# A decoder layer on one Trainium2 core: gather and scatter of the experts' tokens as two-part float32r products, four experts at a time

## The chip, the core and the metric

The kernel runs on one core of a Trainium2 chip. The core has a matrix engine (TensorE, in the profile PE, with PEld for the loading of its weights), VectorE (DVE), ScalarE (ACT), GpSimd (POOL), SyncE (SP) and 16 DMA engines that bring data from the chip's memory (HBM). Each engine runs its own queue of instructions in order and waits for the others by semaphores. The metric is the device time of one execution, in microseconds, and smaller is better. Three runs of the kernel before took 1217.1, 1217.46 and 1218.18 us, with a median of 1217.46.

## The reference

The layer works on 256 tokens of 2048 features, all in float32. It runs three mixers (pooling, sparse attention, cross attention), gates them, adds the projected sum to x, and then adds a mixture of 16 experts. The change touches the last part alone, which is:

```python
x = x + hierarchical_moe(rms_norm(x, g_ffn), ...)

# in hierarchical_moe, h: [1, 256, 2048]
w = pg_top * pe_top / jnp.sum(pe_top, axis=-1, keepdims=True)
e_id = g_top[..., None] * EXPERTS_PER_GROUP + e_local
combine = jnp.einsum('bsk,bske->bse', w, jax.nn.one_hot(e_id, N_EXPERTS))
a = jnp.einsum('bsd,edf->bsef', h, w_e_gate)
b = jnp.einsum('bsd,edf->bsef', h, w_e_up)
act = jax.nn.silu(a) * b * combine[..., None]
return jnp.einsum('bsef,efd->bsd', act, w_e_down)
```

Each token has two experts, both out of one group of four. `combine` is zero for the others, so the kernel computes each expert for its own tokens only. The weights of each expert are three float32 matrices of 2048 x 512 or 512 x 2048, 4 MiB each, and 192 MiB for all sixteen.

## The kernel before

**The stages.** Until about 725 us the kernel computes the mixers and the output projection. Their products take activations and weights as two float32r parts, high and low (lines 268 to 270: high times high, high times low, low times high; `split_evac`, lines 113 to 115, makes the parts with a copy on ACT and a subtraction on DVE). Then comes a short router, which ranks the logits and gives each token a place in the lists of its two experts (`slot`, counted from 1, 0 where an expert is not chosen), and after it the expert stage: eight pairs of experts, one after the other (`pair`, line 953). A pair has 128 slots, 64 for each of its two experts. An expert with more tokens than 64 would need further rounds (line 1073).

**A pair.** `pick` (line 894) compares `slot` with 1 to 64 and so makes a selection matrix [token, slot], multiplied by a factor of the token. `Gather` (line 927) multiplies x with the selection that carries the factor `r2` (1 / rms), in plain float32, and so gets the pair's tokens transposed, two of the 16 k-tiles of 128 features at a step (line 946, called line 951 where the program order is kept); DVE multiplies by the gain (line 947). `gemm` (line 963) runs gate and up, 8 weight tiles each, with the gathered tokens as the stationary operand. Sigmoid and two products make `sg`, which is transposed (line 998) into `aT`. The down product (line 1037) takes 8 more weight tiles in four column parts. `scatter` (line 1007) copies each part out (`ob`, line 1009) and multiplies it with the transposed selection `pwT` that carries the combine weights, also in plain float32 (line 1013); DVE adds the result to `y` (line 1015). The first pair gathers while it uses its gate weights, because all tokens must be there first. Of each later pair, four of eight gather steps come before and behind the transposes of `sg` in the pair ahead of it, and the rest beside its own gate product.

**The weights.** SP loads them in the order of use, one tile of 1 MiB per DMA (`prefetch`, line 731, and `load`, line 189). A load waits until the last product that read the same buffer is done. The buffers form a ring: four that held hT (`wh`), `NEX` of a pool of their own (`we`), four of the raw weights (`wr`) and two that held merged activations (`wm`). With NEX = 8 the ring has 18 buffers. For the first pass two more are there, `mx1`, which later hold `y`. Two tiles of the first pair (`late`, line 727) have buffers of their own. So 22 tiles are loaded before the first one is used up, and 170 follow as buffers come free.

**The order.** The program is written in the order above, and a scheduler with a model of the engines' times sets the order of each engine's queue from it. Only instructions that are pinned with `keep_in_program_order` stay as written: the loads, and the gather and gate products of the first pair.

Of the kernel before, what the change touches and what calls it, by code (L numbers as in the profile page):

```python
# [11 lines left out]
F32 = mybir.dt.float32  # L12
# [8 lines left out]
P = 128  # L21
# [10 lines left out]
NEX = 8  # L32
# [21 lines left out]
def layer_kernel(tc, x, xT, memT, pos, cst, band, gains, bgate, wmem, wxq, widx, wkqvp, wpg, wgb, wo, wr, we, out):  # L54
# [26 lines left out]
    class Quads:  # L81
        """High and low parts of a [K, tokens] operand, four k-tiles to a tile."""
# [67 lines left out]
    class RowRstd:  # L150
        """1 / rms of the tokens, from the transposed activations: squares summed over the k-tiles,
        then over the partitions by a product with ones."""
# [28 lines left out]
    def gain_split(src, gc, dst, q, ks=slice(0, 4)):  # L181
        """src: [P, 4, S], rows [512 q, 512 q + 512) of the transposed activations."""
        for k in range(ks.start, ks.stop):
            g = cs[:, gc + 4 * q + k : gc + 4 * q + k + 1]
            hi, lo = dst.q[q][:, 0, k], dst.q[q][:, 1, k]
            pin(A.activation(hi, src[:, k], AF.Copy, scale=g))
            pin(V.scalar_tensor_tensor(lo, src[:, k], g, hi, op0=ALU.mult, op1=ALU.subtract))
# [25 lines left out]
    # the weights in the order of their use: [P, k-tiles, n] in DRAM  # L213
# [6 lines left out]
    def feeder():  # L220
        """Loads the weights and splits them into two float32r parts, two k-tiles at a time."""
# [28 lines left out]
    def chunk(n, groups, rate=1, name=None, step=None):  # L250
        """groups: list of (k-tiles, operand, done); n output columns."""
# [27 lines left out]
    def warm(n, z, cols, ps):  # L279
        """Products of zeros that nobody reads: the array's clock is up when the next ones come."""  # L280
# [142 lines left out]
    def head_rstd(srcs, H, name):  # L423
        """srcs[t]: [P, H*HD] -> [P, NT, H] of 1/rms."""
# [12 lines left out]
    def transposes(srcs, dst, engine=None):  # L437
        """srcs: list of [P, 128] blocks; dst [P, n, 128] written through one bank (n <= 4)."""
# [6 lines left out]
    def softmax(ps, nk, bias, out):  # L445
        """ps: [P, 2, nk] logits of two heads; out gets the normalised probabilities in SBUF."""
# [74 lines left out]
    def rotary(dst, src, H, half, tl, t, sub=None):  # L521
        """dst, src: [P, H, 2*half]; tl: four [P, half] tables (cos g1, sin g2, cos g2, sin g1)."""
# [262 lines left out]
    def route_in(n, t, ac):  # L785
# [9 lines left out]
        if n < 3:  # L795
            # four k-tiles side by side in column groups of the array
# [42 lines left out]
    c_w, wk = pool("work", side="right")  # L839
    # two tiles of the first weights stay where later the results of their products go  # L840
# [22 lines left out]
    # rank of a logit in its group of four, equal ones in the order of their places; the logits are  # L863
    # those up to the token's positive factor r2; group 0 holds the group logits
# [18 lines left out]
    # place of a token in its expert's list, counted from 1; 0 where the expert is not chosen  # L883
# [10 lines left out]
    def pick(wp, pr, slot_, name, f, bufs=1):  # L894
        """[token, slot] selection of the pair's tokens, times the token's factor f(t, expert)."""
        v = wp.tile([P, NT, P], F32, tag=name, name=name, bufs=bufs)
        for t in range(NT):
            for e in range(2):
                k = 2 * pr + e
# [267 lines left out]
```

## Time and profile before

| | |
|---|---|
| median of three runs | 1217.46 us |
| span of the profiled execution, first to last instruction | 1215.5 us |
| what lies around the span, as the difference of these two | 1.96 us |
| TensorE busy | 1193.3 us, 98% of the span |
| VectorE, ScalarE, GpSimd busy | 546.6, 400.4 and 30.2 us |
| moved by DMA | 340.35 MB, 280 GB/s in the mean |
| expert stage | about 725 to 1207 us |

The profile holds one execution, and it gives a span and no other time of that execution. A busy share of TensorE counts the time in which at least one product is under way, and products overlap in its pipeline: the length of one instruction is not what it costs in a row of many. What it costs there is the distance from one start to the next, which the timeline shows where it merges a run of like instructions and gives their count. A float32 product stands in the trace as two instructions, and a float32r product as one.

### The profile page before, as it was taken

The numbers are of one execution on the slowest core, as the hardware profiler recorded it, in microseconds if no ns is written. First come the engines' busy times: TensorE is split into PE (matmuls) and PEld (weight loads), VectorE is DVE, ScalarE is ACT, GpSimd is POOL, SyncE is SP. The second block draws the span as 40 slices with busy tenths as digits, with TensorE's granted clock in tenths as the row PEclk, the third lists the DMA queues.
The fourth block names the chain that finished last, engine by engine and source line by source line (L and its number), as shares of the span: only waits on it lengthen the run. The fifth ranks groups of instructions, "written<-read, shape, count | busy, mean of one in ns | idle before, by whom it ended". The sixth has DMA issues, their size and how long they took to land. (4 is left out here: it accounts for less than half of the span.)

```text
span 1215.5 us, 15075 instructions
## 1 busy us (share of the span) xinstructions
PE 1193.3 (98%) x6079; PEld 814.7 (67%) x6079; DVE 546.6 (45%) x905; ACT 400.4 (33%) x604; POOL 30.2 (2%) x33
## 2 busy tenths in 40 slices
PE   8999999999999999999999999999999999999996
PEld 5788887888788888888887774545454545453533
DVE  7877469856465565565563541222121212121201
ACT  7765664456544444444444430100000000000000
POOL 4200000000000000000000000000000000000000
PEclk9999999999999999999999999999999999999998
DMA  9646454544745565555797488899999999999951
GB/s 379 208 149 216 173 181 145 201 165 158 256 161 207 183 215 192 206 193 206 300 360 308 173 311 324 338 379 426 405 425 380 426 427 425 422 425 425 427 225 72
DMA packets 49901, 340.35 MB, mean 280 GB/s; under 512 B 5665, under 2 KB 6305, under 8 KB 10401
## 3 DMA queue, kind: packets, MB, share of 16 engines
q1 hardware_dynamic: 46512, 329.83, 70.0%
q0 software_dynamic: 1728, 7.15, 1.7%
q10 hardware_dynamic: 1584, 2.34, 0.5%
q8 instruction: 50, 0.82, 0.3%
q14 instruction: 27, 0.21, 0.0%
HBM read 337.20 MB, written 2.10 MB: 279 GB/s over the span
## 5 line engine op out<-in xcount | busy, mean ns | idle before, releaser
L115 DVE TENSOR_TENSOR wl<-rawt,wh 128x1024 fp32r<-128x1024 f32 (+1 forms) x240 | 292.3, 1220 | 211.5 <-ACT wh L114 210.7
L114 ACT ACTIVATE wh<-rawt 128x1024 fp32r<-128x1024 f32 (+1 forms) x240 | 251.0, 1048 | 296.9 <-PE acc L270 291.4
L269 PE MATMUL acc<-wl,hT 128*128 128x512 f32 (+1 forms) x640 | 249.7, 390 | 0.7 <-DVE wl L115 0.7
L270 PE MATMUL acc<-wh,hT 128*128 128x512 f32 (+1 forms) x640 | 247.3, 387 | 0.0
L268 PE MATMUL acc<-wh,hT 128*128 128x512 f32 (+1 forms) x640 | 228.5, 390 | 0.0
L269 PEld LDWEIGHTS acc<-wl,hT 128*128 128x128 f32 x640 | 120.2, 188 | 25.1 <-DVE wl L115 1.1
L270 PEld LDWEIGHTS acc<-wh,hT 128*128 128x128 f32 x640 | 120.2, 188 | 23.1
L268 PEld LDWEIGHTS acc<-wh,hT 128*128 128x128 f32 x640 | 119.2, 188 | 23.5 <-issue 0.3
L972 PE MATMUL gu<-we,xg 128*64 128x512 f32 x464 | 108.1, 596 | 0.0
L1015 DVE TENSOR_TENSOR y<-y,sm 128x512 f32<-128x512 f32 (+1 forms) x58 | 38.9, 670 | 134.7 <-PE sm L1013 134.7
L972 PEld LDWEIGHTS gu<-we,xg 128*64 128x64 f32 x464 | 33.1, 137 | 58.7 <-issue 56.9
L1009 ACT ACTIVATE ob<-dn 128x512 f32<-128x512 f32 (+1 forms) x33 | 19.3, 585 | 157.6 <-PE dn L1037 153.0
L946 PEld LDWEIGHTS sm<-pg,x 128*128 128x128 f32 x448 | 53.5, 192 | 21.5 <-issue 21.5
L1013 PE MATMUL sm<-ob,pwT 128*128 128x512 f32 (+1 forms) x132 | 63.8, 605 | 0.5 <-ACT ob L1009 0.5
L947 DVE TENSOR_TENSOR xg<-sm,cs 128x256 f32<-128x256 f32 x64 | 26.6, 423 | 72.5 <-PE sm L946 51.9
L946 PE MATMUL sm<-pg,x 128*128 128x128 f32 x448 | 58.7, 280 | 0.0
L972 PE MATMUL gu<-wr,xg 128*64 128x512 f32 x216 | 51.5, 595 | 0.0
L269 PE MATMUL acc<-wl,mgT 128*128 128x512 f32 x128 | 51.4, 402 | 0.0
L270 PE MATMUL acc<-wh,mgT 128*128 128x512 f32 x128 | 50.7, 396 | 0.0
L268 PE MATMUL acc<-wh,mgT 128*128 128x512 f32 x128 | 46.7, 397 | 0.0
L1037 PE MATMUL dn<-we,aT 128*64 128x256 f32 x384 | 45.3, 382 | 0.0
L992 DVE TENSOR_TENSOR sgm<-sgm,gu 128x512 f32<-128x512 f32 x8 | 5.5, 689 | 87.1 <-PE gu L972 87.1
(334 smaller groups left out, 1244.6 us busy)
## 6 DMA issues: line engine op xcount, KB each, us to landing
we<-in_we_dram SPq DMA_DIRECT2D x85, 1024.0 KB, 9.8
rawt<-in_wgb_dram SPq DMA_DIRECT2D x64, 1024.0 KB, 4.7
wh<-in_we_dram SPq DMA_DIRECT2D x44, 1024.0 KB, 9.7
wr<-in_we_dram SPq DMA_DIRECT2D x40, 1024.0 KB, 10.1
rawt<-in_wkqvp_dram SPq DMA_DIRECT2D x24, 1024.0 KB, 4.7
wm<-in_we_dram SPq DMA_DIRECT2D x22, 1024.0 KB, 9.2
rawt<-in_wo_dram SPq DMA_DIRECT2D x16, 1024.0 KB, 4.8
rawt<-in_wmem_dram SPq DMA_DIRECT2D x7, 1024.0 KB, 8.4
```

What stands on the lines that cost most here:

```text
L114: pin(A.activation(hi, ps, AF.Copy))
L115: pin(V.tensor_sub(lo, ps, hi))
L268: mm(o, hi[:, c], wh[:, kk], start=f, stop=False)
L269: mm(o, hi[:, c], wl[:, kk], start=False, stop=False)
L270: mm(o, lo[:, c], wh[:, kk], start=False, stop=l)
L946: self.pe(ps[:, kk], x2[:, t, k * P : (k + 1) * P], self.pg[:, t], start=t == 0, stop=t == NT - 1)
L947: V.tensor_mul(self.xg[:, 2 * b : 2 * b + 2], ps, gf[:, 2 * b : 2 * b + 2].unsqueeze(2).to_broadcast([P, 2, P]))
L972: mm_(ac[64 * e : 64 * e + 64], ga.xg[:, k, 64 * e : 64 * e + 64], w[:, 2 * kk + e], start=k == 0, stop=k == KD - 1)
L1009: A.activation(ob, ad, AF.Copy)
L1013: mm(ps, pwT[:, t * P : (t + 1) * P], ob, start=True, stop=True)
L1015: V.tensor_add(ys, base(t)[:, c0 : c0 + n], ps)
L1037: mm(ad[64 * e : 64 * e + 64, 256 * i : 256 * i + 256], aT[:, k, 64 * e : 64 * e + 64], w[:, k, 256 * e : 256 * e + 256], start=k == 0, st ...
```

## The change

The selection is a plain 0/1 matrix in float32r (`sel`), one for four experts (256 slots) instead of one for two. x is split into two float32r parts as the gather goes on (`split`: a copy on ACT, a subtraction on DVE, three buffers), and a k-tile is gathered by four float32r products of 256 columns (two parts, two token tiles). The factors no longer ride on the selections: a product of `sel` with a table `cw` of the tokens' factors gives each slot its factors (`fac`), 1 / rms and 1 / rms times the combine weight, and these are applied in the sigmoid and in the two products that make `sg`. The transposed selection (`selT`) is made once for four experts, in `back`, and the scatter multiplies it with two float32r parts of `ob`. The gather of the next four experts runs in the second pair of a four, two steps around the transposes and the rest beside the down product. The gathered tokens, parts and selections take more room, and NEX is 6. Comments are dropped, so that lines below shift little.

```diff
@@ -29,7 +29,7 @@
-NEX = 8
+NEX = 6
...
-    def pick(wp, pr, slot_, name, f, bufs=1):
-        """[token, slot] selection of the pair's tokens, times the token's factor f(t, expert)."""
-        v = wp.tile([P, NT, P], F32, tag=name, name=name, bufs=bufs)
-        for t in range(NT):
-            for e in range(2):
-                k = 2 * pr + e
-                V.tensor_scalar(v[:, t, e * 64 : e * 64 + 64], cs[:, C_IOTA : C_IOTA + 64], slot_[:, t, k : k + 1], f(t, k),
-                                op0=ALU.is_equal, op1=ALU.mult)
-        return v
-
-    def pick_in(pr, slot_):
-        return pick(wk, pr, slot_, "pg", lambda t, k: r2[:, t : t + 1])
...
-    pg0 = pick_in(0, slot)
...
+    cwf = rt([P, NT, 18], "cwf")
+    cw = wk.tile([P, 2, NT, 18], F32R, name="cw")
+    V.tensor_mul(cwf[:, :, 0:NE], cmb, r2.unsqueeze(2).to_broadcast([P, NT, NE]))
+    V.tensor_copy(cwf[:, :, NE : NE + 2], r2.unsqueeze(2).to_broadcast([P, NT, 2]))
+    V.tensor_copy(cw[:, 0], cwf)
+    V.tensor_sub(cw[:, 1], cwf, cw[:, 0])
...
+    EQ = 4
+    SQ = EQ * 64
...
     class Gather:
-        def __init__(self, pr, slot_, pg=None):
-            self.pg = pg or pick_in(pr, slot_)
-            self.pe = pe if pg is not None else mm
+        def __init__(self, q, slot_, first=False):
+            self.q = q
+            self.pe = pe if first else mm
+            self.sel = wk.tile([P, NT, EQ, 64], F32R, tag="sel", name="sel")
+            V.tensor_tensor(
+                self.sel,
+                cs[:, C_IOTA : C_IOTA + 64].unsqueeze(1).unsqueeze(1).to_broadcast([P, NT, EQ, 64]),
+                slot_[:, :, EQ * q : EQ * q + EQ].unsqueeze(3).to_broadcast([P, NT, EQ, 64]),
+                op=ALU.is_equal)
+            self.flat = self.sel.rearrange("p t e s -> p t (e s)")
...
+        def split(self):
+            if self.next == KD:
+                return
+            k = self.next
+            self.next += 1
+            xs = wk.tile([P, 2, NT, P], F32R, tag="xs", name="xs", bufs=3)
+            src = x2[:, :, k * P : (k + 1) * P]
+            A.activation(xs[:, 0], src, AF.Copy)
+            V.tensor_sub(xs[:, 1], src, xs[:, 0])
+            self.parts.append(xs)
...
         def step(self):
...
-                self.xg = wk.tile([P, KD, P], F32, tag="xg", name="xg")
-            ps = sm_tile([P, 2, P])
+                self.xg = wk.tile([P, KD, SQ], F32, tag="xg", name="xg")
+            ps = sm_tile([P, 2, SQ])
             for kk in range(2):
-                k = 2 * b + kk
+                while len(self.parts) < 2 and self.next < KD:
+                    self.split()
+                xs = self.parts.popleft()
                 for t in range(NT):
-                    self.pe(ps[:, kk], x2[:, t, k * P : (k + 1) * P], self.pg[:, t], start=t == 0, stop=t == NT - 1)
-            V.tensor_mul(self.xg[:, 2 * b : 2 * b + 2], ps, gf[:, 2 * b : 2 * b + 2].unsqueeze(2).to_broadcast([P, 2, P]))
+                    for h in range(2):
+                        self.pe(ps[:, kk], xs[:, h, t], self.flat[:, t], start=t + h == 0, stop=t + h == 2)
+            V.tensor_mul(self.xg[:, 2 * b : 2 * b + 2], ps, gf[:, 2 * b : 2 * b + 2].unsqueeze(2).to_broadcast([P, 2, SQ]))
+        def back(self, wp):
+            self.selT = wp.tile([P, 2, S], F32R, tag="selT", name="selT", bufs=2)
+            ps = sm_tile([P, 2, NT, P])
+            for h in range(2):
+                for t in range(NT):
+                    nc.tensor.transpose(ps[:, h, t], self.flat[:, t, h * P : (h + 1) * P].bitcast(F32), ident)
+            A.activation(self.selT, ps.rearrange("p h t q -> p h (t q)"), AF.Copy)
+            ps = sm_tile([P, 2, 18])
+            for h in range(2):
+                for t in range(NT):
+                    for u in range(2):
+                        mm(ps[:, h], self.flat[:, t, h * P : (h + 1) * P], cw[:, u, t], start=t + u == 0, stop=t + u == 2)
+            self.f = wp.tile([P, 2, 2], F32, tag="fac", name="fac", bufs=2)
+            for h in range(2):
+                V.tensor_copy(self.f[:, h, 0:1], ps[:, h, NE : NE + 1])
+                for e in range(2):
+                    c = EQ * self.q + 2 * h + e
+                    V.tensor_copy(self.f[64 * e : 64 * e + 64, h, 1:2], ps[64 * e : 64 * e + 64, h, c : c + 1])
...
-    def pair(pr, slot_, base, store, ga):
-        def scatter_in():
-            pwT = pools["w2"][1].tile([P, S], F32, tag="pwT", name="pwT", bufs=2)
-            pw = pick(pools["w2"][1], pr, slot_, "pw", lambda t, k: cmb[:, t, k : k + 1])
-            ps = sm_tile([P, NT, P])
-            for t in range(NT):
-                nc.tensor.transpose(ps[:, t], pw[:, t], ident)
-            A.activation(pwT, ps.rearrange("p t q -> p (t q)"), AF.Copy)
-            return pwT
+    def pair(pr, slot_, base, store, ga, first=False):
+        hf = pr % 2
...
-                        mm_(ac[64 * e : 64 * e + 64], ga.xg[:, k, 64 * e : 64 * e + 64], w[:, 2 * kk + e],
+                        s0 = hf * P + 64 * e
+                        mm_(ac[64 * e : 64 * e + 64], ga.xg[:, k, s0 : s0 + 64], w[:, 2 * kk + e],
...
-        ag = gemm(ga.pe, ahead_)
-        pwT = scatter_in()
-        nx = None if store else Gather(pr + 1, slot_)
+        ag = gemm(ga.pe if hf == 0 else mm, ahead_)
         w2 = pools["w2"][1]
+        if hf == 0:
+            ga.back(w2)
+        nx = ga
+        if hf and not store:
+            nx = Gather(pr // 2 + 1, slot_)
+        r2s, c1s = ga.f[:, hf, 0:1], ga.f[:, hf, 1:2]
         sg = w2.tile([P, FF], F32, tag="sg", name="sgm")
-        A.activation(sg, ag, AF.Sigmoid)
-        V.tensor_mul(sg, sg, ag)
+        A.activation(sg, ag, AF.Sigmoid, scale=r2s)
+        V.scalar_tensor_tensor(sg, ag, r2s, sg, op0=ALU.mult, op1=ALU.mult)
         au = gemm(mm)
-        V.tensor_mul(sg, sg, au)
-        if nx:
-            nx.step()
+        V.scalar_tensor_tensor(sg, sg, c1s, au, op0=ALU.mult, op1=ALU.mult)
+        if nx is not ga:
             nx.step()
...
-            nx.step()
+        if nx is not ga:
             nx.step()
...
         def scatter(ad, c0, n):
-            ob = w2.tile([P, 512], F32, tag="ob", name="ob", bufs=2)[:, :n]
-            A.activation(ob, ad, AF.Copy)
+            ob = w2.tile([P, 2, 512], F32R, tag="ob", name="ob", bufs=2)[:, :, :n]
+            A.activation(ob[:, 0], ad, AF.Copy)
+            V.tensor_sub(ob[:, 1], ad, ob[:, 0])
             yield
             for t in range(NT):
                 ps = sm_tile([P, 512])[:, :n]
-                mm(ps, pwT[:, t * P : (t + 1) * P], ob, start=True, stop=True)
+                for u in range(2):
+                    mm(ps, ga.selT[:, hf, t * P : (t + 1) * P], ob[:, u], start=u == 0, stop=u == 1)
...
                 finish()
+                if nx is not ga:
+                    nx.step()
...
-    ga = Gather(0, slot, pg0)
+    ga = Gather(0, slot, True)
```

What this does to the order of the queues is shown at three places.

On SP, one turn of the ring of weight buffers in the expert stage, before and then after. The names are the buffers that a load fills.

```order
L190 DMA wh<-in_we_dram 128x2048 x4
L190 DMA we<-in_we_dram 128x2048 x8
L190 DMA wr<-in_we_dram 128x2048
L190 DMA wm<-in_we_dram 128x2048
L190 DMA wr<-in_we_dram 128x2048
L190 DMA wm<-in_we_dram 128x2048
L190 DMA wr<-in_we_dram 128x2048 x2
```

```order
L190 DMA wh<-in_we_dram 128x2048 x4
L190 DMA we<-in_we_dram 128x2048 x6
L190 DMA wr<-in_we_dram 128x2048
L190 DMA wm<-in_we_dram 128x2048
L190 DMA wr<-in_we_dram 128x2048
L190 DMA wm<-in_we_dram 128x2048
L190 DMA wr<-in_we_dram 128x2048 x2
```

A turn is 16 loads instead of 18.

On TensorE, the end of the first pair's up product, the transposes of `sg` and the start of its down product (`dn`), before and then after.

```order
L972 MATMUL gu<-wr,xg 64x512 x4
L972 MATMUL gu<-wm,xg 64x512 x4
L959 MATMUL sm<-ident,pw 128x128
L946 MATMUL sm<-pg,x_4892 128x128 x3
L959 MATMUL sm<-ident,pw 128x128
L946 MATMUL sm<-pg,x_4892 128x128 x5
L998 MATMUL sm<-ident,sgm 128x128 x4
L946 MATMUL sm<-pg,x_4892 128x128 x8
L1037 MATMUL dn<-wr,aT 64x256 x8
```

```order
L1006 MATMUL gu<-wr,xg 64x512 x4
L1006 MATMUL gu<-wm,xg 64x512 x4
L1035 MATMUL sm<-ident,sgm 128x128 x4
L1075 MATMUL dn<-wr,aT 64x256 x8
L1075 MATMUL dn<-wm,aT 64x256 x8
```

The gather of the second pair, which stood on both sides of the transposes, is gone from there.

On VectorE, the router's ranking up to the first selection (`pg` before, `sel` after), before and then after, where `xs` is a part of x.

```order
L876 TENSOR_TENSOR wrt<-wrt 128x160
L147 TENSOR_TENSOR r_5650<-r_5650,r2t 128x2
L877 TENSOR_TENSOR wrt<-wrt,cs 128x160
L144 TENSOR_TENSOR r2t<-r_5650 128x2
L878 TENSOR_TENSOR wrt<-wrt 128x160
L145 TENSOR_TENSOR r2t<-r2t,r2s 128x2
L879 TENSOR_REDUCE wrt<-wrt 128x40
```

```order
L876 TENSOR_TENSOR wrt<-wrt 128x160
L147 TENSOR_TENSOR r_5646<-r_5646,r2t 128x2
L950 TENSOR_TENSOR xs<-x_4892,xs 128x256
L877 TENSOR_TENSOR wrt<-wrt,cs 128x160
L950 TENSOR_TENSOR xs<-x_4892,xs 128x256
L144 TENSOR_TENSOR r2t<-r_5646 128x2
L950 TENSOR_TENSOR xs<-x_4892,xs 128x256
L878 TENSOR_TENSOR wrt<-wrt 128x160
L145 TENSOR_TENSOR r2t<-r2t,r2s 128x2
L879 TENSOR_REDUCE wrt<-wrt 128x40
```

Three splits now stand inside the ranking, ahead of the selection.

## Rows read from the trace of the kernel before

**Rows 1.** The page, busy shares, and GB/s in forty slices.

```profile
PE 1193.3 (98%) x6079; PEld 814.7 (67%) x6079; DVE 546.6 (45%) x905; ACT 400.4 (33%) x604; POOL 30.2 (2%) x33
GB/s 379 208 149 216 173 181 145 201 165 158 256 161 207 183 215 192 206 193 206 300 360 308 173 311 324 338 379 426 405 425 380 426 427 425 422 425 425 427 225 72
```

**Rows 2.** Windows: busy us per engine (instructions), clock, DMA share, GB/s.

```profile
725.00:760.00 35.00, 34.49 (x182) 16.02 (x182) 7.61 (x28) 3.42 (x5) 0.00 (x0) 1.00 0.84 331
760.00:790.00 30.00, 30.00 (x205) 17.39 (x203) 7.49 (x16) 3.38 (x6) 0.00 (x0) 1.00 0.87 338
790.00:820.00 30.00, 30.00 (x147) 13.18 (x145) 6.25 (x20) 0.98 (x2) 0.00 (x0) 1.00 0.97 378
960.00:1160.00 200.00, 197.62 (x1151) 96.63 (x1151) 41.49 (x88) 13.48 (x24) 0.00 (x0) 1.00 1.01 425
1170.00:1175.00 5.00, 5.00 (x26) 1.67 (x24) 0.00 (x0) 0.00 (x0) 0.00 (x0) 1.00 0.23 93
```

**Rows 3.** Waits of the queue of SP, 820 to 1216: total us, times, longest.

```profile
SPq L190 <- PE gu L972: 167.9, 88, 5.2
```

**Rows 4.** Timeline of TensorE: the last pair, its wait without filler and its end.

```profile
1181.88 0.66 PE L998 MATMUL sm<-ident,sgm 128*128 128x128 f32 x4 [0.79 <-DVE sgm L992]
1183.22 5.40 PE L1037 MATMUL dn<-wh,aT 128*64 128x256 f32 x48 [0.69 <-ACT aT L1000]
...
1201.50 1.08 PE L1037 MATMUL dn<-we,aT 128*64 128x256 f32 x8
```

**Rows 5.** Timeline of TensorE: gather, down product, scatter; start, us, and count.

```profile
946.35 1.95 PE L946 MATMUL sm<-pg,x 128*128 128x128 f32 x16
948.23 1.95 PE L1037 MATMUL dn<-wr,aT 128*64 128x256 f32 x16
...
953.56 1.98 PE L1013 MATMUL sm<-ob,pwT 128*128 128x512 f32 x4
955.48 1.95 PE L1037 MATMUL dn<-wm,aT 128*64 128x256 f32 x16
```

**Rows 6.** Groups of the expert stage: count, busy us, mean ns, idle before.

```profile
L1013 PE MATMUL sm<-ob,pwT 128*128 128x512 f32 (+1 forms) x132 | 63.8, 605 | 0.5 <-ACT ob L1009 0.5
L946 PE MATMUL sm<-pg,x 128*128 128x128 f32 x448 | 58.7, 280 | 0.0
L946 PEld LDWEIGHTS sm<-pg,x 128*128 128x128 f32 x448 | 53.5, 192 | 21.5 <-issue 21.5
```

**Rows 7.** Timeline of TensorE: split products of 512 and of 324 columns.

```profile
689.62 0.40 PE L268 MATMUL acc<-wh,mgT 128*128 128x512 f32 x1
689.85 0.40 PE L269 MATMUL acc<-wl,mgT 128*128 128x512 f32 x1
...
85.67 0.31 PE L269 MATMUL acc<-wl,hT 128*128 128x324 f32 x1
85.82 0.31 PE L270 MATMUL acc<-wh,hT 128*128 128x324 f32 x1
```

**Rows 8.** Timeline of VectorE, the first two gain products.

```profile
727.60 0.83 DVE L947 TENSOR_TENSOR xg<-sm,cs 128x256 f32<-128x256 f32 x2
```

**Rows 9.** Timeline of TensorE: the first pair and the start of the second.

```profile
728.08 1.94 PE L951 MATMUL gu<-wh,xg 128*64 128x512 f32 x8
...
787.57 0.64 PE L972 MATMUL gu<-wh,xg 128*64 128x512 f32 x1
```

**Rows 10.** Timeline of SP, the first load that waited for a used-up tile.

```profile
730.05 0.33 SPq L190 DMA_DIRECT2D wh<-in_we_dram  x1
```

**Rows 11.** The page, loads of an earlier stage: us to landing.

```profile
rawt<-in_wgb_dram SPq DMA_DIRECT2D x64, 1024.0 KB, 4.7
```

**Rows 12.** Windows with waits of TensorE and what the clock did.

```profile
5.00:10.00 5.00, 3.20 (x10) 1.39 (x9) 2.90 (x5) 4.99 (x8) 0.00 (x0) 1.00 1.04 428
10.00:20.00 10.00, 9.87 (x37) 7.53 (x35) 9.39 (x8) 9.14 (x15) 6.53 (x2) 0.83 1.01 424
720.00:726.00 6.00, 4.04 (x35) 3.61 (x34) 5.06 (x32) 1.86 (x2) 0.00 (x0) 1.00 0.81 299
```

More of the change, by code (lines that the diff above doesn't have):

```diff
@@ L922, in layer_kernel @@
     V.tensor_mul(cmb, cmb, s2.unsqueeze(2).to_broadcast([P, NT, NE]))
+    cwf = rt([P, NT, 18], "cwf")
[4 more added lines that the diff above has]
+    V.tensor_sub(cw[:, 1], cwf, cw[:, 0])
     gf = cs[:, C_GFFN : C_GFFN + KD]
     ys_ = []
+    EQ = 4
+    SQ = EQ * 64
     class Gather:
-        def __init__(self, pr, slot_, pg=None):
-            self.pg = pg or pick_in(pr, slot_)
-            self.pe = pe if pg is not None else mm
-            self.xg = None
-            self.todo = deque(range(8))
+        def __init__(self, q, slot_, first=False):
[8 more added lines that the diff above has]
+            self.flat = self.sel.rearrange("p t e s -> p t (e s)")
+            self.xg = None
+            self.parts = deque()
+            self.next = 0
+            self.todo = deque(range(KD // 2))
+        def split(self):
[8 more added lines that the diff above has]
+            self.parts.append(xs)
         def step(self):
@@ L1000, in pair @@
         A.activation(aT, ps, AF.Copy)
-        if nx:
-            nx.step()
+        if nx is not ga:
             nx.step()
```

## The prediction

> **What bounds the kernel now.** I read the busy shares of the page first. TensorE is busy for 98% of the span, and no other engine for half of it [rows 1]. The change touches only the expert stage, so I went on to the windows of that stage. Each of them has TensorE busy for nearly all of its length. But the windows show a second thing at its limit: the DMA share is 1.01 at 425 GB/s from 960 to 1160, and it was only 0.84 to 0.97 before 820 [rows 2]. So two resources are full side by side, and the question is what a faster TensorE meets. Next came the waits of SP's queue, which issues the weight loads. From 820 on it waited 167.9 us for gate and up products that still read a buffer [rows 3]. The stream is thus held by the ring of buffers as well as by its own rate. The loads end at about 1171, since the window from 1170 to 1175 moves 93 GB/s, about a fifth of the full rate [rows 2]. The last tile is not used before 1201.50 [rows 4]. TensorE ends about 30 us behind the stream, and today it sets the end.
>
> **What TensorE saves.** Prices are distances between starts. A gather pass of 128 columns costs 1.88 us over 16 = 0.118, and a scatter pass of 512 columns costs 1.92 over 4 = 0.48 [rows 5]. A float32 product has two passes.
> - Gather before: 8 pairs x 16 k-tiles x 2 token tiles = 256 products, 512 passes (448 in the one group, the first pair's 64 under another line) [rows 6], so 60.2 us. Gather after: 4 x 16 x 4 = 256 products in float32r with 256 columns. The trace has float32r with 512 columns at 0.23 and with 324 columns at 0.15 [rows 7], so the straight line through both gives about 0.12 at 256. The lower bound is the 0.118 of a gather pass. The upper bound is two float32 passes of 256 columns, 0.48 by half the scatter's price. I take 0.12, because float32r rows are the nearest: 30.7 us, a saving of 29.5.
> - Scatter before: 64 products, 128 full passes at 0.48 (the 132 of the group include the split last part) [rows 6], so 61.4 us. After: 128 float32r products at 0.23, 29.4 us. It saves 32.0.
> - Added: 8 products of 18 columns for each four experts to get the factors, at no more than a 128-column pass, 32 x 0.12 = 3.8 us. Transposes of the selection stay at 16.
> - The wait for `sg`: in the last pair of before nothing fills it, and TensorE idles 0.79 ahead of the transposes and 0.69 behind them [rows 4]. Now the first pair of each four has nothing there either. In the first pair of all both idle times are new, 1.5 us. In the four pairs together I count 3.
> - The start: DVE does three splits inside the ranking, a fourth ahead of the first gain product, and instructions on `cw`. A split reads as many columns as an old gain product, 0.83 over 2 = 0.42 [rows 8], so 1.7 us, and I add 0.6 for the rest as an estimate. The first weight product, at 728.08 before [rows 9], starts 2.3 later. The bounds are 0, if the splits fall into DVE's gaps, and 3.
>
> TensorE alone would end 29.5 + 32.0 - 3.8 - 3 - 2.3 = 52.4 us sooner, at a span of 1163. DVE, less than half busy, hides the other splits (64 for x, 33 for `ob`), and ACT hides its copies. SP's register load for the rounds moves by two loads of its queue, and waits for a count that is known soon after the first pair: I cost it at nothing.
>
> **What the stream allows.** A tile of 1.049 MB at 425 GB/s takes 2.47 us [rows 2]. With NEX = 6 only 20 tiles instead of 22 are loaded before the first is used up, so 172 remain. The first of these was issued at 730.05 before [rows 10], hence at 732.3 now. If it never waited again, the stream would end at 732.3 + 172 x 2.47 = 1157. It does wait, though. The load of the 41st tile needs the buffer of the 25th, which is the first tile of the second pair. So I need the length of the first pair, 787.57 - 728.08 = 59.5 us before [rows 9]. In it were ten gather steps of 8 passes (six of its own, four for the second pair), 9.4 us, and now six of 8 products, 5.8. Three of its scatter parts save 1.0 each. The factors and two more transposes add 1.2, and the bare wait for `sg` 1.5. That makes 59.5 - 3.6 - 3.0 + 1.2 + 1.5 = 55.6. The second pair starts at 728.1 + 2.3 + 55.6 = 786.0, and its first tile is used up 1.9 later. A load on a quiet queue lands 4.7 us after its issue [rows 11], so the 41st tile lands at 792.6. From there TensorE gains on the stream in each pair and the buffers come free in time: 151 tiles x 2.47 = 373, and the last lands at 1165.6.
>
> From the start of the last tile's products to the end of the span were 14.0 us (1215.5 - 1201.50) [rows 4]. The shorter scatter and the longer making of `ob` about cancel there. The span is then 1179.6. The profiled execution has only its span, and the median of the runs stands 1.96 above it. I carry that over: 1181.5, say 1181 us, 3% faster.
>
> A rule speaks against the price of 2.47. The Trainium skill's "DMA: Bandwidth & Descriptors", section "Where 436 GB/s comes from", has transfers from HBM bound at about 358 GB/s for a core. By it a tile would take 2.93 us, 151 of them 442, and the kernel would come out above 1245. The trace disagrees, with 425 GB/s held for 200 us, so the sum stays with the trace and the rule gets no chance of its own.
>
> **The rivals.**
> - *The stream loses as much as before.* Until 820 it ran at 331, 338 and 378 GB/s [rows 2], which against 425 is 7.7 + 6.1 + 3.3 = 17 us lost. If the first pair frees no sooner, the end of 1171 moves back by two tiles and the late start, 4.9 + 2.3, and the kernel takes 1178.3 + 14 + 2 = 1194. For it speaks that the first gate product holds as many gather instructions as before. Against it: all else in that pair gets shorter.
> - *TensorE stays the bound.* In the second pair of each four the gather steps stand in rows of 9 to 12 products. A step takes 8 x 0.12 = 0.96 on TensorE, but two splits and a gain product of twice the columns on DVE, some 1.5 us. All 32 steps at DVE's pace cost 18 us more, and a span of 1181.5. If the weight loads, 0.192 each [rows 6], are not hidden either and scatter waits behind splits in DVE's queue, it reaches 1200. Against it: half of the steps have weight products between them.
> - *The clock falls.* Once TensorE waits for tiles, it idles for a part of each 2.47 us. From 5 to 10 us it was busy 3.20 of 5 while DMA was full, and the granted clock then fell, to a mean of 0.83 in the next 10 us. But it stayed at 1.00 from 720 to 726, where TensorE was busy for 4.04 of 6 [rows 12]. Here it would be busy for some 90%, and a fall to 1.2 GHz makes it busier still. A quarter of the last 100 us at half speed costs 12 us, so 1193. [...]
> - *Slower.* If float32r with 256 columns runs no faster than float32, a gather product costs the upper 0.48, and the gather 123 us instead of 60.2. TensorE then needs 62.7 - 32.0 + 9.1 = 40 us more, and the kernel takes 1257. The mechanism decides from 0.33 us a product on, where 256 of them eat what the scatter saves. The 324 columns at 0.15 speak against it. The change would not do what it says for the gather.
>
> **How the numbers follow.** The stream as worked out, 1171 to 1190: 0.67. Losses as before, 1194: 0.10. TensorE the bound, 1183 to 1200: 0.11. The clock, near 1193: 0.05. Slower, 1257: 0.05. The remaining 0.02 is no difference, which means within 0.2%, about what a measurement of this kernel can tell. Its lower end follows from the stream without early waits, 1157 + 14 + 2 = 1173, and a rate a little above 425; I go to 1169. Its upper end takes in the losing stream and most of the bound TensorE, 1198. Faster by over 0.2%: 0.93. Slower by over 0.2%: 0.05.
>
> **What would show it.** In the profile of the changed kernel a run of gather products should stand 0.12 apart and of scatter products 0.23. DMA should be full from about 800 us on and stop near 1166. TensorE should wait for loads (gate, up or down products released by DMA) in the last two or three pairs, and its last tile should start within 1 us of its landing. The first weight product should stand near 730.4 and the second pair near 786. The prediction is wrong if TensorE still waits for no load, if DMA ends as late as 1175 or later, or if the gather products stand more than 0.2 apart.

## The result, and the profile after

The changed kernel takes 1200.94 us (median; 1200.78 to 1201.83) against 1217.28 us of the kernel before on the same chip: a ratio of 0.9867, with an interval from 0.9854 to 0.988. It is faster by 16 us. The forecast was 36 us, and the time lies above the range. The span of the profiled execution is 1200.0 us.

The page answers to [rows 1 and 6]: busy shares, GB/s in forty slices, and the group of the scatter (count, busy us, mean ns, idle before).

```profile
PE 1163.4 (97%) x5855; PEld 791.5 (66%) x5855; DVE 575.7 (48%) x938; ACT 425.9 (35%) x664; POOL 30.1 (3%) x33
...
GB/s 384 206 147 228 176 155 170 175 176 185 202 192 204 187 215 190 206 197 209 285 289 335 167 269 203 401 345 426 375 427 426 426 426 426 427 426 426 425 426 184
...
L1051 PE MATMUL sm<-ob,selT 128*128 128x512 f32 (+1 forms) x132 | 45.7, 433 | 8.5 <-ACT ob L1045 8.0
```

TensorE is still busy for 97%. The scatter has as many instructions as before, and now 8.5 us of waits ahead of them, where [rows 6] had 0.5.

The windows answer to [rows 2 and 12].

```profile
725.00:760.00 35.00, 34.56 (x151) 16.24 (x151) 13.49 (x43) 7.63 (x17) 0.00 (x0) 0.91 0.59 221
760.00:790.00 30.00, 28.47 (x186) 14.47 (x184) 8.15 (x19) 5.79 (x9) 0.00 (x0) 1.00 0.91 366
790.00:820.00 30.00, 30.00 (x144) 11.13 (x142) 6.19 (x14) 2.12 (x4) 0.00 (x0) 1.00 0.99 399
960.00:1160.00 200.00, 191.59 (x1081) 86.09 (x1081) 47.19 (x88) 20.49 (x39) 0.00 (x0) 1.00 1.01 426
1175.00:1180.00 5.00, 4.24 (x30) 2.14 (x28) 1.52 (x3) 0.60 (x1) 0.00 (x0) 1.00 0.80 325
720.00:726.00 6.00, 4.95 (x24) 4.55 (x23) 4.78 (x29) 1.51 (x4) 0.44 (x2) 0.60 1.02 403
```

The stream is full from 820 on, as it was to be, but it ends at 1182 and not at 1166. TensorE's clock, at 1.00 in the router before, is at 0.60 there now. The waits of SP's queue from 820 on answer to [rows 3]:

```profile
SPq L190 <- PE gu L1006: 68.0, 52, 4.2
SPq L190 <- DMA we<-in_we_dram: 61.1, 33, 3.6
SPq L190 <- PE dn L1075: 57.2, 24, 4.4
```

The waits for gate and up products are down from 167.9 to 68.0 us, and a load now often waits for another load. The last pair on TensorE answers to [rows 4]:

```profile
1165.58 0.66 PE L1035 MATMUL sm<-ident,sgm 128*128 128x128 f32 x4 [0.85 <-DVE sgm L1030]
1166.92 5.40 PE L1075 MATMUL dn<-we,aT 128*64 128x256 f32 x48 [0.69 <-ACT aT L1037]
...
1182.01 0.74 PE L1051 MATMUL sm<-ob,selT 128*128 128x512 f32 x2 [0.76 <-ACT ob L1045]
...
1186.17 1.95 PE L1075 MATMUL dn<-wm,aT 128*64 128x256 f32 x16 [0.50 <-DVE ob L1046]
```

It waits for `sg`, `aT` and `ob`, and for no load: in the whole expert stage no product waits for one. Only the loading of the array's weights (PEld), which goes on beside the products, waits for loads, 5.9 us in 19 waits of at most 0.4. The last tile lands at about 1182 and is used from 1186.2. So TensorE still sets the end, 4 us behind the stream instead of 28.

What it does in the middle of the stage answers to [rows 5]: down products and the scatter of the third pair, then down products, gather and scatter of the fourth.

```profile
893.57 1.19 PE L1051 MATMUL sm<-ob,selT 128*128 128x512 f32 x4
894.70 1.95 PE L1075 MATMUL dn<-wr,aT 128*64 128x256 f32 x16
897.40 0.73 PE L1051 MATMUL sm<-ob,selT 128*128 128x512 f32 x2 [0.76 <-ACT ob L1045]
898.06 1.95 PE L1075 MATMUL dn<-wh,aT 128*64 128x256 f32 x16
899.94 0.73 PE L1051 MATMUL sm<-ob,selT 128*128 128x512 f32 x2
...
940.49 1.68 PE L966 MATMUL sm<-sel,xs 128*128 128x256 f32 x12
942.09 1.95 PE L1075 MATMUL dn<-we,aT 128*64 128x256 f32 x16
...
957.11 0.76 PE L966 MATMUL sm<-sel,xs 128*128 128x256 f32 x5
957.71 0.62 PE L1051 MATMUL sm<-ob,selT 128*128 128x512 f32 x2
958.26 1.51 PE L1075 MATMUL dn<-we,aT 128*64 128x256 f32 x10
959.70 0.63 PE L966 MATMUL sm<-sel,xs 128*128 128x256 f32 x3
```

Three things stand here. Twelve gather products take 1.60 us, 0.133 each. A visit of two scatter products takes 0.66 us, not 0.46. And most parts are scattered in two visits (59 visits in the whole trace, against 33 before); where the first stands directly behind the last down product of its own part, TensorE idles 0.7 us until `ob` is copied. Before, a part was scattered in one visit, about one weight tile later.

To see where the time went I added up, over all records of the trace from the first gate product to the last product, the distance from each product's start to the next one's, by kind, with idle time apart (us; the first 16 gather products lie ahead of it):

| | before | after |
|---|---|---|
| gather | 61.7 | 35.6 |
| scatter | 60.5 | 40.3 |
| down | 115.2 | 123.7 |
| gate and up | 227.9 | 229.7 |
| factors, transposes, rest | 6.7 | 9.8 |
| idle behind down products (`ob`) | 0.5 | 8.0 |
| idle elsewhere (`sg` and `aT` above all) | 5.5 | 11.6 |
| sum | 478.0 | 458.7 |

Gather and scatter give 46.3 us. Of these 27 come back: 8.5 in the down products, which more visits interrupt, 13.6 in new waits, 3.1 in the factors and 1.8 in gate and up.

### The profile page after: what moved, and what is told of

Its sections match the earlier page's. It is cut to its first block, busy times and chain, and to the rows that moved or that the text cites. A ratio compares the mean times of both kernels' runs of the same rounds, so it can differ in the third digit from the quotient of the medians.

```text
span 1200.0 us, 14718 instructions
## 1 busy us (share of the span) xinstructions
PE 1163.4 (97%) x5855; PEld 791.5 (66%) x5855; DVE 575.7 (48%) x938; ACT 425.9 (35%) x664; POOL 30.1 (3%) x33
## 4 chain that ended last, share of the span: by engine, by line
PE 93%; DVE 3%; ACT 2%; issue 1%; DMA 0%; DVEq 0%; ACTq 0%
PE gu L1006 18%; PE acc L269 17%; PE acc L270 17%; PE acc L268 17%; PE dn L1075 10%; PE sm L1051 3%; PE sm L966 2%; PE gu L991 1%; PE sm L991 1%; PE sm L442 1%; PE sm L686 1%; DVE wl L115 1%; ACT ob L1045 1%; DVE memT L187 1%; DVE sgm L1030 1%
## 5 line engine op out<-in xcount | busy, mean ns | idle before, releaser
L1006 PE MATMUL gu<-we,xg 128*64 128x512 f32 x368 | 86.2, 596 | 0.0
L1045 ACT ACTIVATE ob<-dn 128x512 fp32r<-128x512 f32 (+1 forms) x33 | 19.3, 584 | 123.2 <-PE dn L1075 123.2
L1006 PE MATMUL gu<-wr,xg 128*64 128x512 f32 x240 | 58.9, 593 | 0.0
L1006 PEld LDWEIGHTS gu<-we,xg 128*64 128x64 f32 x368 | 26.0, 137 | 48.1 <-issue 44.7
L1051 PE MATMUL sm<-ob,selT 128*128 128x512 f32 (+1 forms) x132 | 45.7, 433 | 8.5 <-ACT ob L1045 8.0
L949 ACT ACTIVATE xs<-x 128x256 fp32r<-128x256 f32 x64 | 26.3, 416 | 74.7 <-PE sm L966 45.9
L1046 DVE TENSOR_TENSOR ob<-dn,ob 128x512 fp32r<-128x512 f32 (+1 forms) x33 | 22.2, 674 | 58.8 <-ACT ob L1045 58.8
L1006 PE MATMUL gu<-wh,xg 128*64 128x512 f32 x224 | 49.3, 592 | 0.0
L1075 PE MATMUL dn<-we,aT 128*64 128x256 f32 x384 | 48.2, 386 | 0.7 <-ACT aT L1037 0.7
L1030 DVE SCALAR_TENSOR_TENSOR sgm<-sgm,fac,gu 128x512 f32<-128x512 f32 x8 | 6.0, 747 | 87.8 <-PE gu L1006 87.8
```

What stands on the lines that cost most here:

```text
L949: A.activation(xs[:, 0], src, AF.Copy)
L1006: mm_(ac[64 * e : 64 * e + 64], ga.xg[:, k, s0 : s0 + 64], w[:, 2 * kk + e], start=k == 0, stop=k == KD - 1)
L1045: A.activation(ob[:, 0], ad, AF.Copy)
L1051: mm(ps, ga.selT[:, hf, t * P : (t + 1) * P], ob[:, u], start=u == 0, stop=u == 1)
L1075: mm(ad[64 * e : 64 * e + 64, 256 * i : 256 * i + 256], aT[:, k, 64 * e : 64 * e + 64], w[:, k, 256 * e : 256 * e + 256], start=k == 0, st ...
```

## The experiments

Three theories stood. *The order*: float32r products are as cheap as priced, but the scheduler set them in more and shorter visits, with waits, and the rest is given back there. *The price*: a product between others never is as cheap as in a long run. *The stream*: the shorter ring, or the loads, hide the gain.

**All products in program order.** In the changed kernel every product of the expert stage is pinned (they then carry line 991). The gather, five other groups of products and two groups of transposes change like this:

```diff
-                    mm(ps, ga.selT[:, hf, t * P : (t + 1) * P], ob[:, u], start=u == 0, stop=u == 1)
+                    pe(ps, ga.selT[:, hf, t * P : (t + 1) * P], ob[:, u], start=u == 0, stop=u == 1)
```

> The changed kernel with every TensorE product of the expert stage kept in program order, so the four products of a scatter part stand together, one weight tile behind their part. Theory (the order that the scheduler chose took back the gain: some 59 visits to the scatter instead of 32, 8 us of waits for ob, broken runs of gate, up and down products): TensorE needs about 20 to 25 us less from the first gate product to the last down product, the stream then ends about 1178 and sets the end, and the time is 1190 to 1196. Rival (switching between float32 and float32r products costs as much in any order, or the stream already sets the end): 1198 or more.

It takes 1188.75 us, a ratio of 0.9764 (0.9748 to 0.978) to before: 12 us less with the same work. TensorE, in the third pair's down stage and in the last pair:

```profile
880.88 1.90 PE L991 MATMUL dn<-wm,aT 128*64 128x256 f32 x16
882.60 1.90 PE L991 MATMUL dn<-wr,aT 128*64 128x256 f32 x16
884.43 1.21 PE L991 MATMUL sm<-ob,selT 128*128 128x512 f32 x4
885.57 1.95 PE L991 MATMUL dn<-wr,aT 128*64 128x256 f32 x16
887.35 1.90 PE L991 MATMUL dn<-wh,aT 128*64 128x256 f32 x16
...
1129.57 1.94 PE L991 MATMUL gu<-wr,xg 128*64 128x512 f32 x8 [0.50 <-DMA wr<-in_we_dram]
1132.00 1.94 PE L991 MATMUL gu<-wm,xg 128*64 128x512 f32 x8 [0.49 <-DMA wm<-in_we_dram]
```

Four scatter products in a visit take 1.14 us, and from 1127 on, in the last pair's gate and up products, each weight tile is waited for as it lands. That is the state that the prediction described, reached only here.

Added up as in the table above, the ordered kernel has 117.9 us in down products, 225.2 in gate and up, 37.7 in the scatter (32 visits) and 34.1 in the gather, together 14.4 less than the changed kernel. It still waits 6.8 us for `ob`, where the changed kernel waits 9.0, since the last part of a pair has no weight tile behind it to cover its copy:

```profile
785.58 1.95 PE L991 MATMUL dn<-wh,aT 128*64 128x256 f32 x16
788.23 0.50 PE L991 MATMUL sm<-ob,selT 128*128 128x512 f32 x1 [0.70 <-ACT ob L1045]
```

So what the order gave back lies in the broken runs, and only a small part in the waits for `ob`.

**The control: program order alone.** The same pins in the kernel before.

```diff
-            self.pe = pe if pg is not None else mm
+            self.pe = pe
...
-                mm(ps, pwT[:, t * P : (t + 1) * P], ob, start=True, stop=True)
+                pe(ps, pwT[:, t * P : (t + 1) * P], ob, start=True, stop=True)
```

> The kernel before with every TensorE product of its expert stage kept in program order. Theory (its scheduled order already has the scatter products of a part together and nothing to win): within 4 us of the kernel before, 1213 to 1221. Rival (program order is worth some 10 us by itself, whatever the products): 1208 or less.

1220.72 us, a ratio of 1.0021 (1.0012 to 1.0031), so a little slower. Program order is no gain by itself, and it brings the same waits at the end of each pair: 5.3 us for `ob`, where the kernel before has 0.5. In the changed kernel it is worth 12 us in spite of them.

**The ring alone.**

```diff
-NEX = 8
+NEX = 6
```

> The kernel before with a ring of 16 buffers instead of 18 (NEX 6), nothing else. Theory (the ring only sets how far the stream leads, and its loads still end 20 us ahead of TensorE): 1216 to 1220. Rival (the shorter ring holds the products up and hides a part of the change's gain): 1225 or more.

1217.84 us, 1.0001 (0.9991 to 1.001). The shorter ring costs nothing where TensorE ends well behind the stream: there the last tile landed 24 us ahead of its use instead of 28.

**The scatter undone, in the scheduler's order and in program order.** `selT` and `ob` in plain float32, one product for two:

```diff
-                for u in range(2):
-                    mm(ps, ga.selT[:, hf, t * P : (t + 1) * P], ob[:, u], start=u == 0, stop=u == 1)
+                mm(ps, ga.selT[:, hf, t * P : (t + 1) * P], ob, start=True, stop=True)
```

> The changed kernel with its scatter back in plain float32, one product of two passes, a single copy for ob. Theory (counted with its switches and waits the scatter gained only some 9.5 us): 1207 to 1213. Rival (the prediction's price, 32 us for the scatter): 1225 or more.

1210.32 us (0.9936, 0.9919 to 0.9952), 9.4 us more than the changed kernel, or 8.4 by the two ratios. So the scatter's half of the change brought about 9 us, where the prediction had 32. The group of the scatter:

```profile
L1049 PE MATMUL sm<-ob,selT 128*128 128x512 f32 (+1 forms) x132 | 63.4, 603 | 0.5 <-ACT ob L1045 0.5
```

With passes in float32 the scheduler left almost no wait ahead of the scatter, 0.5 us against 8.5. Then the same in program order:

> The fully ordered kernel with its scatter back in plain float32. TensorE waited about 9 us for loads in the fully ordered kernel, so that much of its loss is covered. Theory (a scatter in float32r still pays the ways in and out, so that in order it is worth some 3.6 us for two pairs, 14 in all): the stretch from the fourth to the sixth pair grows from 109.4 to about 113 us and the kernel takes 1191 to 1197. Rival (in good order the float32r scatter is worth the prediction's 32 us): the stretch grows to 117 and the kernel takes 1208 or more.

1201.36 us (0.9868, 0.9852 to 0.9885), 12.6 us more than the ordered kernel. The stretch of two pairs is 114.7 us instead of 109.4, which lies between the two expectations. 5.3 us for two pairs are 21 in all; 12.6 of them are left in the time, and loads take most of the rest: the ordered kernel waits 5.9 us for them, and this one not at all. So in order the scatter is worth about 21 us of TensorE's time: more than I thought after the first result, and two thirds of the predicted 32. Most of the rest is the price of a short visit: one of four products takes 1.14 us and not 0.92, 7 us over 32 visits.

**Only down and scatter products in order.**

```diff
-                        mm(ad[64 * e : 64 * e + 64, 256 * i : 256 * i + 256], aT[:, k, 64 * e : 64 * e + 64],
+                        pe(ad[64 * e : 64 * e + 64, 256 * i : 256 * i + 256], aT[:, k, 64 * e : 64 * e + 64],
```

> The changed kernel with only the down and the scatter products kept in program order; gate, up, gather and transposes stay with the scheduler. Theory (what the order took back lies around the scatter: visits of two products instead of four, waits for ob, broken runs of down products): most of the 12 us of the fully ordered kernel comes back, 1189 to 1194. Rival (the loss lies in the gather's short runs among gate and up products): 1196 to 1200.

1194.25 us (0.9807, 0.9791 to 0.9823): 6.7 of the 12.2 us, just outside what I expected. TensorE is as fast in the middle as with all in order (108.6 us from the fourth pair to the sixth, and 109.4). But up products of the first pair still stand among its gate and gather products, and gate products of the second pair ahead of the first pair's last down tile: it starts at 794.7 instead of 785.6. SP's queue is in order, so all loads behind it wait, and the 41st tile lands at 804.1 instead of 796.8. TensorE waits for loads in the last pair here too, and I put the other 5.5 us down to that delay, which no run tested by itself.

**Two visits for a part.** The scatter generator yields after the first token tile:

```diff
+                if t == 0:
+                    yield
```

> The fully ordered kernel, but the two token tiles of each scatter part in two visits, one behind each of the next two weight tiles; as many products as before. The number to look at is the third pair's second neighbour, the stretch from the start of the fourth pair to the start of the sixth, where no load is waited for: 109.4 us in the fully ordered kernel. Theory (each further visit costs about 0.4 us: the way in 0.2, the way out 0.1, the first product 0.1): 8 visits more, about 112 to 113 us, and the kernel takes up to 5 us longer than the fully ordered one. Rival (a visit costs nothing, only the waits for ob did): 109 to 110 us.

1191.23 us (0.978, 0.9764 to 0.9797), and the stretch is 110.4 us: 1.0 more, not 3.2. The count of visits was wrong: the stretch has 12 instead of 8, not 16, because at the end of a pair, where no weight tile is left, the last products stand in one visit. Four visits at the 0.33 us worked out below make 1.3. Visits of two products:

```profile
886.01 1.95 PE L991 MATMUL dn<-wr,aT 128*64 128x256 f32 x16
887.89 0.73 PE L991 MATMUL sm<-ob,selT 128*128 128x512 f32 x2
888.55 1.95 PE L991 MATMUL dn<-wh,aT 128*64 128x256 f32 x16
```

From one weight tile to the next are 2.54 us (888.55 - 886.01). Two tiles on end stand 1.72 apart (882.60 - 880.88 in the ordered kernel, above), so a visit of two products costs 0.82 us, and a visit of four there costs 885.57 - 882.60 - 1.72 = 1.25, and 0.06 in the tile behind it. Two visits cost 0.33 more than one.

**Half of the scatter left out.** In program order, the products with the low part of `ob` are not made (which changes the output).

```diff
-                for u in range(2):
-                    pe(ps, ga.selT[:, hf, t * P : (t + 1) * P], ob[:, u], start=u == 0, stop=u == 1)
+                pe(ps, ga.selT[:, hf, t * P : (t + 1) * P], ob[:, 0], start=True, stop=True)
```

> The fully ordered kernel without the scatter products of the low part of ob (64 of 128 products left out; the parts are still made). TensorE has some 15 us less to do. Theory (with the products in order the stream of weight loads sets the end, as the prediction had it): the time falls only by what the first pair gets shorter, 1 to 2 us, to 1186 to 1189. Rival (TensorE still sets the end): 1172 to 1180.

1187.41 us (0.9747, 0.973 to 0.9763), 1.3 us less for some 15 us less of work. Windows from 960 to 1160, of the ordered kernel and of this one:

```profile
960.00:1160.00 200.00, 187.10 (x1074) 83.86 (x1072) 41.53 (x78) 19.22 (x36) 0.00 (x0) 1.00 1.01 426
```

```profile
960.00:1160.00 200.00, 176.75 (x1006) 74.37 (x1004) 41.05 (x78) 18.82 (x35) 0.00 (x0) 1.00 1.01 426
```

DMA moves the same while TensorE is busy for 10 us less, and TensorE's waits for loads grow from 5.9 to 18 us in all. In the ordered kernel TensorE is the bound no longer; the loads are.

**The start.** In the ordered kernel:

```diff
-            V.tensor_sub(xs[:, 1], src, xs[:, 0])
+            d = V.tensor_sub(xs[:, 1], src, xs[:, 0])
+            if self.first:
+                tc.keep_in_program_order(d)
...
-    warm(2, ident, P, wps)
+    warm(8, ident, P, wps)
```

> The fully ordered kernel with the first splits of x kept behind the router's ranking on VectorE, and eight warming products instead of two in the router. Theory (the splits inside the ranking and the clock at 0.5 from 722.8 to 729.6 make the first weight product late, and where the stream sets the end each us at the start counts in full): the first gate product starts 1.5 to 3 us sooner, the time falls to 1185.5 to 1187.5. Rival (the start is hidden by the loads): 1188 to 1189.5.

A miss: 1189.23 us (0.9762, 0.9746 to 0.9778), no gain. The first gate product starts at 731.6, later than the 730.5 of the ordered kernel:

```profile
725.59 3.35 PE L282 MATMUL warm<-ident 128*128 128x128 f32 x16
728.70 1.80 PE L994 MATMUL sm<-sel,xs 128*128 128x256 f32 x13
731.10 0.62 PE L994 MATMUL sm<-sel,xs 128*128 128x256 f32 x3 [0.60 <-DVE xs L951]
```

The selection was ready at 726.7, and the added products, at half clock themselves, held TensorE until 728.70. As two things were changed at once, the run doesn't tell what the splits alone cost, nor whether an earlier start would be worth its time. That stays open.

**A longer ring, and larger gather blocks.** In the ordered kernel one late tile instead of two, and with its room (and single buffers for `ob`, `selT`, and `sg` with `aT`) one buffer more in the ring:

```diff
-NEX = 6
+NEX = 7
...
-    late = [(0, 6), (0, 7)]
+    late = [(0, 7)]
```

> The fully ordered kernel with a ring of 17 buffers instead of 16 (NEX 7) and one late tile instead of two, so that one more buffer of the first pair's gate product goes back into the ring; the room comes from single buffers for ob, selT and for sg with aT. Theory (from the first pair on the stream never catches up what it loses there: between 747.5 and 755.5 no load was issued because the two late tiles free nothing): the hole shrinks by one tile, all later loads land 1.5 to 2.5 us sooner, and the kernel takes 1186 to 1187.5. Rival (TensorE sets the end, or single buffers hold it up): 1188.5 or more.

1187.45 us (0.9752, 0.9736 to 0.9768), 1.3 us less, at the edge of what was expected. Windows from 745 to 760, of the ordered kernel and of this one:

```profile
745.00:760.00 15.00, 15.00 (x81) 6.51 (x82) 4.92 (x14) 4.24 (x7) 0.00 (x0) 1.00 0.66 232
```

```profile
745.00:760.00 15.00, 15.00 (x81) 6.65 (x81) 4.91 (x14) 4.24 (x7) 0.00 (x0) 1.00 0.88 304
```

The hole in the stream shrinks, 66% to 88% busy, and the last tile lands 2.3 us sooner, at 1170.95. Last, gather in blocks of two steps on top:

```diff
-            while 8 - len(ga.todo) < min(8, i + 2):
+            while 8 - len(ga.todo) < min(8, 2 + 2 * ((i + 1) // 2)):
```

> The kernel with the longer ring, and in the first pair's gate product the gather goes in blocks of two steps (16 products) instead of one. Theory (a way from weight products to gather products and back costs 0.4 us, three fewer, and the first pair sets the stream): another 1 us less, 1185 to 1186.5. Rival (VectorE's splits are too slow for blocks of 16, so TensorE waits in them): no gain on the longer ring alone, or a loss.

1188.66 us (0.976, 0.9744 to 0.9776): no gain. The rival held; each block of 16 waits for a split:

```profile
732.36 1.82 PE L991 MATMUL sm<-sel,xs 128*128 128x256 f32 x13
734.70 0.62 PE L991 MATMUL sm<-sel,xs 128*128 128x256 f32 x3 [0.52 <-DVE xs L950]
```

The best version run is thus the ordered kernel with the longer ring, 1187.45 us, though its 1.3 us to the ordered one are about the spread of the runs of either.

## Why the prediction was wrong, point by point

**The step that failed** is "TensorE alone would end ... 52.4 us sooner". The span is 15.5 us shorter. From its first gate product to its last product TensorE saved 19.3 us and not 54.7. So the stream could not become the bound, and the sum was made on the wrong one of the two. The term that fell shortest is the scatter's 32.0, of which about 9 were left; the order of the products had been put at nothing. By its terms:

- *Gather, 29.5 us*: 26.1 by the table. The price of 0.12 held in a run; short runs of 3 to 9 products took the rest. The prediction had the steps in rows of 9 to 12 beside the down product; only nine runs of the trace are that long.
- *Scatter, 32.0*: 20.2 in its own products. The price of 0.23 was that of a long run [rows 7], while the old price was that of a visit of four passes [rows 5]. A visit of two new products costs 0.66 and one of four 1.14, against 0.46 and 0.92. Good order doesn't take this away: the ordered kernel got 21 of the 32.
- *What nothing was charged for*: the order itself. More ways in and out cost the down products 8.5 us, and idle time for `ob` rose by 7.5. The ordered kernel got 5.8 of the first back and little of the second. The undone scatter shows what is left of the 32: about 9 us. The rows from the order of the changed kernel looked at loads, transposes and the ranking. Where the scatter now stood had not been read, and it was there to be read.
- *Factors, 3.8*: 4.0. *The wait for `sg`, 3*: about 5 with that for `aT`.
- *The start, 2.3*: 3.1. The first gate product starts at 731.22. The splits in the ranking are as foreseen. New is that the clock was at half from 721.2 to 731.5, so that 16 gather products took 3.8 us and not 1.9. Kernels without the change had this fall too (see the last section), so the prediction was near here in part by luck:

```profile
727.41 3.88 PE L991 MATMUL sm<-sel,xs 128*128 128x256 f32 x16
731.22 2.03 PE L991 MATMUL gu<-wh,xg 128*64 128x512 f32 x8
...
792.92 0.64 PE L1006 MATMUL gu<-we,xg 128*64 128x512 f32 x1
```

- *The first pair, 55.6*: 62 us here and 59.4 in order. The ways between gate and gather products, and up products among them, were not priced. So the load of the 41st tile was issued 8.2 us later than reckoned (796.13), and it took 7.1 us instead of 4.7 on a queue that wasn't quiet: the tile landed at 803.2, not 792.6.
- *The stream from there on* was right: 151 tiles in 378.6 us are 2.51 each against 2.47, and at 1.01 of DMA's share. From the last tile's products to the end are 13.8 us, against 14.0.

**The rivals.** "TensorE stays the bound" came true, with a time just above its range of 1183 to 1200, and by another mechanism than I gave: not VectorE's pace in the gather (in the unpinned gather no product waited for `xs`, and the loading of its weights waited 1.9 us) but the scatter's visits and the order. "The clock falls" did not hold where I put it: in the ordered kernel TensorE waited about half a us for each tile from 1127 on, and the clock stayed at 1.00:

```profile
1125.00:1155.00 30.00, 23.70 (x102) 6.27 (x98) 1.50 (x2) 0.69 (x1) 0.00 (x0) 1.00 1.01 426
```

"Slower" is refuted: products of 256 columns stand 0.12 to 0.14 apart.

With the order repaired, the prediction's mechanism held. The loads set the end; the 41st tile landed at 796.8 and the last at 1173.2, 7.6 us behind the forecast: 4.2 from the 41st tile, and 3.4 because the next 151 landed 2.49 apart and not 2.47, the last of them in two halves that took 3.8. 1188.75 us is inside the range.

## What to carry to other kernels

Price a short visit as a whole, with its first product, its way in and its way out, and not by the distance inside a long run: the cheaper a product, the more of its cost lies at the edges. Where a scheduler sets the order, read where the cheaper instructions now stand, for it may move them next to what they wait for; undoing half of the change and pinning the order shows what each is worth. And when two resources end within a few per cent of each other, a saving on one ends at the other: in the ordered kernel 15 us less of TensorE's work were worth 1.3 us.

## What the runs showed of the hardware

- The edge of a visit. Inside a run of scatter products the distance is 0.232 us (median of the ordered kernel, without the first of a visit). The first takes 0.34 to the next, and its weight load starts with it (both at 884.43 in the visit shown above) and not ahead of it; the last takes 0.33 to the first down product. The scatter stands 0.31 behind the start of the last down product, and the next gather product 0.52 behind the start of the last gate product. The edges have the same size in plain float32: in the kernel before (medians of its 33 visits) the ways in are 0.31 and 0.52 too, the first pass takes 0.53 and the last 0.52, where a pass inside takes 0.43. So they do not come from the change between float32 and float32r, which was the rival of the first experiment. The Trainium skill, "TensorEngine Tiling (Array Packing)", section "Key Properties", says that a change of the tiling mode drains the engine. Down and gate products write 64 columns of the array and scatter and gather all 128, so these distances agree with it, but no run here changed the mode alone.
- The clock in the router. It was at 1.00 in the kernel before with TensorE busy for 4.04 of 6 us [rows 12], and at 0.60 here with 4.95 of 6 busy, which half clock itself makes longer. All eleven kernels of the experiments had a fall between 721 and 732 too, among them the kernel before with the shorter ring and the one with pins. So it comes without the change as well; why it came in these and not in the first profile stays open. The longer row of warming products started at 725.59, when the clock had been down since 721.5, and it stayed down until 728.4.
